# S5 boundary states stored contiguous by chunk, and some second copies moved from ScalarE to VectorE

## The chip, the cores and the metric

The kernel runs on one core of a Trainium2 chip. The metric is the device time of one execution in microseconds, as the median over several runs. TensorE (PE) multiplies matrices, VectorE (DVE) and ScalarE (ACT) work element by element, GpSimd (POOL) does so too and starts DMAs, SyncE (SP) starts most of the DMAs. In the profile PE stands for products, PEld for the loading of their stationary matrices.

## The reference, cut to what matters

A backbone of two layers is applied to 128 context tokens and 256 latent tokens. Each layer is half a SwiGLU feed-forward, a token mixer, and half a feed-forward. The mixer of the first layer is an S5 state-space layer: 64 groups of 16 channels, each with 64 complex states, scanned in both directions.

```python
def s5_mixer(h, p, j, init):
    ...
    u = (h @ w_in[j]).astype(F32)
    ug = u.reshape(bt, l, S5_GROUPS, S5_GROUP)
    for d, rev in ((0, False), (1, True)):
        abr, abi, bbr, bbi = s5_discretize(...)
        ...
        sr, si = s5_direction(ug, abr, abi, bbr, bbi, s0, rev)   # s[t] = A s[t-1] + B u[t]
    ...
    y = (jnp.einsum('blgp,gip->blgi', s_re, c_re[j].astype(F32))
         - jnp.einsum('blgp,gip->blgi', s_im, c_im[j].astype(F32)))
    y = y.reshape(bt, l, D_MODEL) + d_skip[j].astype(F32) * u
    y = jax.nn.gelu(y).astype(h.dtype)
    a, g = jnp.split(y @ w_glu[j], 2, axis=-1)
    out = a * jax.nn.sigmoid(g)
```

## The kernel before, in words

All activations lie with channels on the partitions and tokens on the free axis, 384 tokens side by side. Large products are split into a high and a low part (`hi` by ACT, `lo` by DVE) and take three products each, at lines L263 to L265; their weights come through seven buffers `raw` of 512 KB that SP loads in the written order (`fetched`, L245).

The S5 mixer cuts the tokens into chunks of 8: 16 of the context, 32 of the latents, and one column of zeros between them, so `NC_` = 49 chunk columns. The work has these steps.

1. The input projection gives U, [(t, j), group, chunk], by way of DRAM (`ud`), with DMAs that POOL starts.
2. `inputs(b)`, L861, multiplies U by a matrix for each group; ACT and DVE copy the results into `sb`, [state, slot, re/im, group], in an order in which both directions run forward (rows 0 to 63 are the forward direction, 64 to 127 the backward one).
3. `steps` (L878 to L881) runs the recurrence over chunks in `sb`, 32 steps of four operations for three blocks of groups: DVE takes groups 0 to 23, then 40 to 63, and POOL 24 to 39. DVE's two blocks are written as one loop, the third block starting 22 steps after the first.
4. `direct(m)`, L909, multiplies a chunk's own inputs and puts the result of eight groups in one bank of PSUM. `m` counts the eight groups of groups. `twice` lets each product write a second time into columns that are not used.
5. `align` copies boundary states from `sb` into `al[m]`, eight groups to a tile: `first_part(m)` what the first sixteen steps give, `second_part(m)` the rest, two copies of 240 and 528 columns on 64 partitions each. All are on ACT (`on_act`); the profile gives them L847, the line of `on_act`. In `al` the columns are [chunk, re/im, group], so a group's 49 chunks lie 16 floats apart.
6. `outputs(m)`, L918, adds the states' part to the bank: 16 products of 64 columns (`CP`), each multiplied twice, so 128 columns. The columns past 49 belong to padding that POOL sets to zero (L890). Then ACT applies the Gelu (L921), and its queue writes y to DRAM (`yd`). This is called y(m) below.
7. `fetch` brings y back by channel, and `split` makes `hh` (ACT, L945) and `hl` (DVE, L947), the input of the GLU product, whose first six weights are split beside y(5) to y(7) and behind.

The order of DVE, ACT and SP in this part is written out by hand: all of `inputs`, all of `direct`, the loop of the recurrence, and then one list of parts, where f is a first part, s_ a second part, y an `outputs`:

```python
for part, m in ((f, 0), (f, 1), (f, 2), (s_, 0), (s_, 1), (y, 0), (s_, 2), (f, 3), (f, 4), (y, 1),
                (s_, 3), (y, 2), (f, 5), (s_, 4), (y, 3), (f, 6), (f, 7), (s_, 5), (y, 4),
                (s_, 6), (y, 5), (s_, 7), (y, 6), (y, 7)):
```

Behind each y(m) of that list stand two more loads of matrices, the `fetch` of y(m-1), the `split` of y(m-3), behind y(5) and y(6) the splitting of GLU weights, and behind y(2) and y(3) a few products of the modulation of a later layer (L143 on TensorE, summed by DVE). Each engine runs its instructions in order.

Of the kernel before, what the change touches and what calls it, by code (L numbers as in the profile page):

```python
# [16 lines left out]
D = 1024  # L17
# [6 lines left out]
Q = 8  # L24
# [20 lines left out]
def backbone(ctx, tc, a, o):  # L45
# [41 lines left out]
    def ada_chunks():  # L87
        """Pieces of the modulation's weights: for TensorE in groups of (kind, pair of tiles) that are transposed
        together, for VectorE by tiles."""
        for l in range(2):  # L90
            for s in range(3):
                groups = [[(0, tp), (1, tp)] for tp in range(4)] if (l, s) == (0, 0) else \
                    [[(kind, tp) for tp in range(4)] for kind in (0, 1)]
                for group in groups + [[(2, tp) for tp in range(4)]]:
                    if (l, s, group[0][0]) in ADA_VEC:
                        vec_todo.extend((l, s, group[0][0], t) for t in range(KT))
                        continue
                    for j in range(len(group)):
                        for kh in range(2):
                            yield l, s, group, j, kh  # L100
# [10 lines left out]
    def ada_room(pool, bufs):  # L111
        """More buffers for pieces loaded ahead, for a while."""
        assert not any(x[2] for x in ada_loaded)
        ada_extra[:] = pool, bufs, 0

    def ada_load(cap=99, q=nc.gpsimd):
        """Loads ahead, up to cap pieces."""
        while ada_todo and len(ada_loaded) < min(cap, ADA_BUFS + ada_extra[1]):
            extra = ada_extra[2] < ada_extra[1]
            pool = ada_extra[0] if extra else adp  # L120
            w = pool.tile([128, 4, 256], F32, name="adaw", tag="adaw", bufs=ada_extra[1] if extra else ADA_BUFS)
            ada_extra[2] += extra
            c = ada_todo.pop(0)
            l, s, group, j, kh = c
            kind, tp = group[j]
            q.dma_start(w, a["ada_w"][l, s, kind * 4 + tp, kh])  # L126
            ada_loaded.append((c, w, extra))

    def ada_fill(n=1, load=True, bank=psaux, flush=True):
        """The products of n loaded pieces of the modulation's weights, then the next loads. Those of a group's  # L130
        item j come in rows 2 j, 2 j + 1 of each quarter, which holds a quarter of the sum."""
# [24 lines left out]
    def vec_pool():  # L156
        """For a while, what ada_vec needs."""
        st = ExitStack()
        vec[3] = vp = phase(st, "vec")
        vec[:2] = vp.tile([128, 2, D], F32, name="cb"), vp.tile([128, 256], mybir.dt.bfloat16, name="dump")  # L160
        nc.sync.dma_start(vec[0], bass.AP(a["condr"].tensor, 0, [[0, 128], [1, 2 * D]]))
        S.activation(vec[0], vec[0], AF.Silu)
        return st

    def ada_vec():
        """A tile of the modulation on VectorE: sums over a quarter of the rows each, then of those."""
# [103 lines left out]
    def pairs(w, n, xh, xl, at={}):  # L270
        """Column-tile pairs (a, g) of products with K = 1024; the tiles of one call go k by k.
        at[k], if given, is called before the products of row tile k."""
# [14 lines left out]
    def singles(w, n, xh, xl, at={}):  # L287
        """Single column tiles of one product with K = 1024; the tiles of one call go k by k."""
        ps = [psum() for _ in w]
        for k in range(KT):  # L290
            if k in at:
                at[k]()
            for i, t in enumerate(w):
                mm3(ps[i][:, :n], t, k * 128, xh[:, k, :n], xl[:, k, :n], k == 0, k == KT - 1)
        return ps

# [1 line left out]
    def params(i, t0=0, t1=KT, out=None):  # L298
        """Affine of norm i - 1 with the shift and scale of sub-layer i, for tiles t0 .. t1."""
# [24 lines left out]
    class Norm:  # L324
        """Norm i of r. Its input's products with the next weights start before the statistics are known:
        W (rs (r - mu) g' + b') = rs (W (g' r)) - rs mu (W g') + W b', for the tiles that come first."""
# [18 lines left out]
        def add(self, m):  # L345
            """Row tile m of r is final."""
# [19 lines left out]
        def pre(self, load, group, srcs, n, then):  # L366
            """The first products of the next sub-layer, n sources at a time, with the statistics in between;
            the weights of the products that follow."""
# [53 lines left out]
        def rest(self):  # L422
            """The input of the next sub-layer, split in hh and hl, and ALPHA * x in r."""
# [8 lines left out]
        def final(self):  # L432
            """The norm itself, to the output."""
# [15 lines left out]
        def apply(self, ps):  # L449
            """The norm on the product of ph, pl in ps, but for its column bias: (tile, biases)."""  # L450
# [97 lines left out]
    # State rows are (direction, p). A backward state's chunks are taken in reverse.  # L548
# [11 lines left out]
    def vexp(out, x, k, p):  # L560
        """exp(x) on the vector engine, to float32's last bits; x, k and p are overwritten."""
# [17 lines left out]
    def s5_tables(gp_):  # L579
        """Generator of the steps that build the chunk matrices."""  # L580
# [13 lines left out]
        # sine and cosine of ang, by quadrant  # L594
# [33 lines left out]
        # powers 0 .. 8 of A  # L628
# [22 lines left out]
        # q = (A - 1) / a  # L651
# [18 lines left out]
        # pe[s]: power 7 - s (forward), s (backward); pg: powers 0 .. 8, - (forward), -, 8 .. 0 (backward)  # L670
# [11 lines left out]
        def build_e(ch):  # L682
# [7 lines left out]
            # bb = q b  # L690
# [4 lines left out]
            # E: [g][ri][s][j]  # L695
# [7 lines left out]
        def build_g(ch, bc, ncr):  # L703
            """C A^e: [g][ri][slot][i]"""
# [26 lines left out]
        def taps(ch, bb, Gt):  # L731
            """[j][slot][i], slots 0 .. 7 backward (lag 7 .. 0), 7 .. 14 forward (lag 0 .. 7), and D"""
# [35 lines left out]
    def beside(slots, n, soon=0, nvec=0):  # L768
        """Work beside the products, called at each of so many slots: n pieces of the modulation on TensorE, evenly
        after the first ones, or, before those, nvec on VectorE, and steps of the S5 tables."""  # L770
# [19 lines left out]
    def s5(i, prev):  # L790
        l, s3 = divmod(i, 3)
        with ExitStack() as st:
            sa = phase(st, "s5a")
            # CP columns or more, as many as cost no more than NC_, are multiplied: those past NC_ are not used,
            # and where they reach into the next result's place that result overwrites them
# [43 lines left out]
            with ExitStack() as st2:  # L839
# [9 lines left out]
                def inputs(b):  # L849
                    """Each chunk's own part of the states: slot c + 1, backward chunks in reverse."""  # L850
# [19 lines left out]
                def steps(E, g0, n):  # L870
                    """The recurrence over chunks for n groups, operation by operation."""
# [11 lines left out]
                # boundary states by chunk, eight groups to a tile  # L883
                al = {}

                def al_tiles():
                    for m in range(8):
                        p_, tag = ((hip, "hi"), (lop, "lo"))[m % 2]
                        al[m] = p_.tile([128, 1024], F32R, name="al", tag=tag).bitcast(F32)
                        G.memset(al[m][:, NC_ * 16:], 0.0)  # L890

                def align(copy, m, c0, n, s0, dr, d):
                    """States d of chunks c0 .. c0 + n from slots s0, s0 + dr, .."""
                    copy(vw(al[m], c0 * 16, [[16, n], [8, 2], [1, 8]], 64 * d, 64),
                         vw(sb, s0 * 128 + m * 8, [[128 * dr, n], [64, 2], [1, 8]], 64 * d, 64))

                def twice(py, g, n):
                    """Group g's place in a bank and one that is not used, for the same again: TensorE's clock stays
                    up, and the columns of the matrices take as long to load."""
                    return vw(py, g * NC_, [[512 - CP - g * NC_, 2], [1, n]])  # L900

                def direct(m):
                    """The part of y from its own chunk: [(t, i), g, c], eight groups to a bank."""
# [9 lines left out]
                def outputs(m, py, gt):  # L913
                    """The states' part of y, and back to channels by tokens."""
                    for g in range(8):
                        for ri in range(2):
                            c0 = ((g % 4) * 2 + ri) * 128
                            PE.matmul(twice(py, g, CP), gt[g // 4][:, c0:c0 + 128],  # L918
                                      vw(al[m], ri * 8 + g, [[0, 2], [16, CP]]), start=False, stop=g == 7 and ri == 1)
# [9 lines left out]
                with tc.manual_schedule(engines={ET.Pool}):  # L929
                    proj(1, False, al_tiles)  # L930
                    with tc.manual_schedule(engines={ET.DVE, ET.Activation, ET.SP}):
                        py, yc = {}, {}

                        def first_part(m):
                            """What the first sixteen steps give of the boundary states."""
# [3 lines left out]
                        def second_part(m):  # L939
                            align(on_act, m, 34, 15, 34, 1, 0)  # L940
                            align(on_act, m, 16, 33, 49, -1, 1)
# [90 lines left out]
    def lru_params():  # L1032
# [6 lines left out]
        # softplus(-lam) = max(-lam, 0) + log1p(exp(-|lam|))  # L1039
# [20 lines left out]
    def lru(i, prev):  # L1060
# [11 lines left out]
        def conv(m, t, b=None):  # L1072
            """Centred convolution along each sequence: the first tap."""
# [5 lines left out]
        def taps(m, t):  # L1079
            """The other taps."""  # L1080
# [37 lines left out]
        def scan(mm, E=V):  # L1118
            w, A, B = ([x[mm, d] for d in range(2)] for x in (W, R, GI))
            # 1 - A^2 = tanh(4 softplus r) (1 + A)^2  # L1120
# [158 lines left out]
    def enter(tp, part=None):  # L1279
        """Rows 2 tp, 2 tp + 1 of the first input, in two parts."""  # L1280
# [14 lines left out]
    def first(load):  # L1295
        """The first products, as their weights, the input and its modulation come in."""
# [123 lines left out]
```

## Time and profile before

| what | value |
|---|---|
| time, median of three runs | 1669.81 us (1669.69 to 1672.33) |
| span of the profiled execution | 1665.7 us |
| TensorE busy, products | 1579.2 us (95%) |
| VectorE busy | 1255.1 us (75%) |
| ScalarE busy | 701.7 us (42%) |
| GpSimd busy | 349.3 us (21%) |
| moved by DMA | 301.23 MB, 181 GB/s on average |

The span is the time from the first to the last instruction of the one execution that was profiled; the device time has some 4 us more around it. A busy share is an average over stages with different limits. A row of a group of instructions has the line, the engine, the operation, output and inputs by name, the shapes, the number, busy time, mean duration in ns, and the idle time of the engine just before with what ended it. A row in order of time has the start, the duration, engine and line, and in brackets the idle time before it.

### The profile page before, as it was taken

What the parts mean: (1) busy time and instruction counts of PE and PEld (TensorE: products, weight loads), DVE (VectorE), ACT (ScalarE), POOL (GpSimd) and SP (SyncE); (2) the same over time, 40 slices, a digit from 0 to 9 for tenths busy, and PEclk for the clock granted to TensorE, in tenths of its full rate; (3) what the DMA queues carried; (4) which work ended last, traced back from release to release, by engine and by line L of the source; (5) the groups of instructions that cost most, each with busy time, mean ns of one, the idle gap of its engine ahead of it and who ended that gap; (6) DMA issues with size and microseconds to landing.
All of it is one profiled execution on the core that took longest, in us unless ns stands there. A gap on an engine that the chain in (4) does not pass through costs nothing.

```text
span 1665.7 us, 26476 instructions
## 1 busy us (share of the span) xinstructions
PE 1579.2 (95%) x9690; PEld 1495.3 (90%) x9690; DVE 1255.1 (75%) x3093; ACT 701.7 (42%) x1166; POOL 349.3 (21%) x553
## 2 busy tenths in 40 slices
PE   6989999999889999999999999999999689999996
PEld 5877987899878998999999999999987589999996
DVE  4999999977583478978769997884587979744444
ACT  4422332346433456333336532333459466333332
POOL 0145445433480004000000400000154513000001
PEclk9999999999989999999999999999999899999997
DMA  9676776875676742757546365654614353544321
GB/s 349 250 229 213 246 237 231 269 242 223 128 261 183 244 140 94 235 173 238 177 138 199 120 200 175 228 182 122 215 64 153 114 165 124 171 148 139 103 75 38
DMA packets 100867, 301.23 MB, mean 181 GB/s; under 512 B 20320, under 2 KB 32096, under 8 KB 100480
## 3 DMA queue, kind: packets, MB, share of 16 engines
q1 hardware_dynamic: 83920, 242.80, 45.0%
q0 software_dynamic: 15664, 55.12, 10.3%
q8 instruction: 76, 1.25, 0.3%
q10 hardware_dynamic: 1152, 1.61, 0.3%
q14 instruction: 55, 0.45, 0.1%
HBM read 275.89 MB, written 27.80 MB: 182 GB/s over the span
## 4 chain that ended last, share of the span: by engine, by line
PE 71%; DVE 18%; DMA 4%; issue 3%; POOL 2%; ACT 2%; SPq 0%; ACTq 0%; DVEq 0%; POOLq 0%
PE mm L263 21%; PE mm L264 21%; PE mm L265 20%; PE mm L918 3%; DVE lo L255 2%; DVE hl L316 1%; PE mm L861 1%; DMA adaw<-in_ada_w 1%; DMA ud<-s5stg 1%; PE aux L143 1%; DVE s5tp L641 1%; PE aux L918 1%; DVE r L427 1%; DVE lxc L1085 1%; DMA s5U<-ud 1%
## 5 line engine op out<-in xcount | busy, mean ns | idle before, releaser
L263 PE MATMUL mm<-hh,hi 128*128 128x384 f32 (+1 forms) x1632 | 561.4, 344 | 12.4 <-DVE hh L1138 5.3
L264 PE MATMUL mm<-hl,hi 128*128 128x384 f32 (+1 forms) x1632 | 555.3, 340 | 14.1 <-DVE hl L316 13.9
L265 PE MATMUL mm<-hh,lo 128*128 128x384 f32 (+1 forms) x1632 | 554.1, 340 | 0.3 <-DVE lo L255 0.3
L255 DVE TENSOR_TENSOR lo<-raw,hi 128x1024 fp32r<-128x1024 f32 (+1 forms) x344 | 390.8, 1140 | 185.7 <-ACT hi L252 179.2
L252 ACT ACTIVATE hi<-raw 128x1024 fp32r<-128x1024 f32 (+1 forms) x332 | 322.2, 975 | 492.3 <-PE mm L264 447.1
L263 PEld LDWEIGHTS mm<-hh,hi 128*128 128x128 f32 x1632 | 308.5, 189 | 30.9 <-issue 16.7
L264 PEld LDWEIGHTS mm<-hl,hi 128*128 128x128 f32 x1632 | 308.5, 189 | 20.3 <-DVE hl L316 19.8
L265 PEld LDWEIGHTS mm<-hh,lo 128*128 128x128 f32 x1632 | 308.4, 189 | 0.8 <-DVE lo L255 0.8
L263 PE MATMUL mm<-zh,hi 128*128 128x384 f32 x704 | 243.7, 346 | 6.0 <-ACT zh L475 6.0
L264 PE MATMUL mm<-zl,hi 128*128 128x384 f32 x704 | 239.5, 340 | 0.5 <-DVE zl L476 0.5
L265 PE MATMUL mm<-zh,lo 128*128 128x384 f32 x704 | 239.1, 340 | 0.0
L263 PEld LDWEIGHTS mm<-zh,hi 128*128 128x128 f32 x704 | 133.2, 189 | 16.2 <-issue 8.8
L264 PEld LDWEIGHTS mm<-zl,hi 128*128 128x128 f32 x704 | 133.3, 189 | 1.5 <-DVE zl L476 1.5
L265 PEld LDWEIGHTS mm<-zh,lo 128*128 128x128 f32 x704 | 133.2, 189 | 0.0
L178 DVE SCALAR_TENSOR_TENSOR dump<-raw,cb 128x256 bf16<-128x256 f32 x256 | 108.5, 424 | 27.1 <-DMA raw<-in_ada_t 26.2
L475 ACT ACTIVATE zh<-w 128x384 fp32r<-128x384 f32 x88 | 46.0, 524 | 183.4 <-DVE w L483 179.6
L178 DVE SCALAR_TENSOR_TENSOR raw<-raw,cb 128x256 f32<-128x256 f32 x256 | 108.4, 424 | 5.6
L126 POOL DMA_DIRECT2D adaw<-in_ada_w x55 | 31.4, 571 | 309.4 <-PE aux L143 286.6
L391 POOL TENSOR_TENSOR t<-mv 128x3 f32<-128x3 f32 x5 | 4.1, 814 | 385.0 <-ACT mv L390 385.0
L540 DVE SCALAR_TENSOR_TENSOR r<-mm,gate,r 128x128 f32<-128x128 f32 (+1 forms) x144 | 53.3, 412 | 24.5 <-PE mm L265 24.3
L429 POOL TENSOR_SCALAR r<-r,lag,lab 128x384 f32<-128x384 f32 x40 | 65.5, 1651 | 24.1 <-ACT w L321 24.0
L476 DVE TENSOR_TENSOR zl<-w,zh 128x384 fp32r<-128x384 f32 x88 | 53.2, 608 | 19.2 <-ACT zh L475 19.0
(357 smaller groups left out, 2039.9 us busy)
## 6 DMA issues: line engine op xcount, KB each, us to landing
raw<-in_up SPq DMA_DIRECT2D x176, 512.0 KB, 4.4
raw<-in_ada_t SPq DMA_DIRECT2D x64, 512.0 KB, 3.9
raw<-in_down SPq DMA_DIRECT2D x56, 512.0 KB, 3.6
adaw<-in_ada_w POOLq DMA_DIRECT2D x55, 512.0 KB, 5.1
adaw<-in_ada_w SPq DMA_DIRECT2D x25, 512.0 KB, 8.1
raw<-in_down SPq DMA_DIRECT2D x48, 192.0 KB, 2.4
gd<-s5G POOLq DMA_DIRECT2D x16, 512.0 KB, 4.6
etd<-s5eo POOLq DMA_DIRECT2D x16, 512.0 KB, 5.5
```

What stands on the lines that cost most here:

```text
L126: q.dma_start(w, a["ada_w"][l, s, kind * 4 + tp, kh])
L178: V.scalar_tensor_tensor(out, wq, 1.0, cb[:, g, q * 256:q * 256 + 256], op0=OP.mult, op1=OP.mult, accum_out=part[:, t, g, q:q + 1])
L252: S.activation(hi[:, :n], raw[:, :n], AF.Copy)
L255: V.tensor_tensor(lo[:, :n], raw[:, :n], hi[:, :n], op=OP.subtract)
L263: PE.matmul(ps, hi[:, c:c + 128], xh, start=start, stop=False)
L264: PE.matmul(ps, hi[:, c:c + 128], xl, start=False, stop=False)
L265: PE.matmul(ps, lo[:, c:c + 128], xh, start=False, stop=stop)
L429: G.tensor_scalar(r[:, k, :], r[:, k, :], lag[:, i, k:k + 1], lab[:, i, k:k + 1], op0=OP.mult, op1=OP.add)
L475: S.activation(zh, z, AF.Copy)
L476: V.tensor_tensor(zl, z, zh, op=OP.subtract)
L540: V.scalar_tensor_tensor(r[:, m, c0:c1], ps[:, c0:c1], gate[:, m, g:g + 1], r[:, m, c0:c1], op0=OP.mult, op1=OP.add)
L918: PE.matmul(twice(py, g, CP), gt[g // 4][:, c0:c0 + 128], vw(al[m], ri * 8 + g, [[0, 2], [16, CP]]), start=False, stop=g == 7 and ri == 1)
```

## The change

`al` is laid out as [re/im, group, chunk], so the 49 chunks of a group lie side by side; `align` stores accordingly. `outputs` multiplies 49 columns, twice, instead of 64, twice, and the padding with its memsets is gone. The second copies of m = 3 to 7 are done by VectorE instead of ScalarE, at the same places of the written order. All other lines of the diff take out comments.

```diff
                 def al_tiles():
                     for m in range(8):
                         p_, tag = ((hip, "hi"), (lop, "lo"))[m % 2]
                         al[m] = p_.tile([128, 1024], F32R, name="al", tag=tag).bitcast(F32)
-                        G.memset(al[m][:, NC_ * 16:], 0.0)
 
                 def align(copy, m, c0, n, s0, dr, d):
-                    copy(vw(al[m], c0 * 16, [[16, n], [8, 2], [1, 8]], 64 * d, 64),
+                    copy(vw(al[m], c0, [[1, n], [8 * NC_, 2], [NC_, 8]], 64 * d, 64),
                          vw(sb, s0 * 128 + m * 8, [[128 * dr, n], [64, 2], [1, 8]], 64 * d, 64))
...
                 def outputs(m, py, gt):
                     for g in range(8):
                         for ri in range(2):
                             c0 = ((g % 4) * 2 + ri) * 128
-                            PE.matmul(twice(py, g, CP), gt[g // 4][:, c0:c0 + 128],
-                                      vw(al[m], ri * 8 + g, [[0, 2], [16, CP]]), start=False, stop=g == 7 and ri == 1)
+                            PE.matmul(twice(py, g, NC_), gt[g // 4][:, c0:c0 + 128],
+                                      vw(al[m], (ri * 8 + g) * NC_, [[0, 2], [1, NC_]]), start=False,
+                                      stop=g == 7 and ri == 1)
...
                         def second_part(m):
-                            align(on_act, m, 34, 15, 34, 1, 0)
-                            align(on_act, m, 16, 33, 49, -1, 1)
+                            copy = on_act if m < 3 else V.tensor_copy
+                            align(copy, m, 34, 15, 34, 1, 0)
+                            align(copy, m, 16, 33, 49, -1, 1)
```

## Rows read from the trace of the kernel before

**Rows 1.** The page: span, and the chain's lines.

```profile
span 1665.7 us, 26476 instructions
...
PE mm L263 21%; PE mm L264 21%; PE mm L265 20%; PE mm L918 3%; DVE lo L255 2%; DVE hl L316 1%; PE mm L861 1%; DMA adaw<-in_ada_w 1%; DMA ud<-s5stg 1%; PE aux L143 1%; DVE s5tp L641 1%; PE aux L918 1%; DVE r L427 1%; DVE lxc L1085 1%; DMA s5U<-ud 1%
```

**Rows 2.** Three stretches: busy us of PE, PEld, DVE, ACT, POOL; clock, DMA.

```profile
475.00:494.00 19.00, 19.00 (x139) 16.45 (x139) 16.70 (x82) 6.41 (x14) 16.57 (x63) 1.00 0.91 320
494.00:515.00 21.00, 21.00 (x98) 19.59 (x96) 16.45 (x86) 7.35 (x13) 7.25 (x28) 1.00 0.63 194
...
539.00:553.00 14.00, 14.00 (x67) 13.24 (x65) 4.72 (x5) 5.83 (x9) 0.00 (x0) 1.00 0.74 210
```

**Rows 3.** The chain in order of time: start, us, what.

```profile
475.62 1.96 PE mm L909 x16
...
494.13 20.96 PE mm L918 x96
515.09 1.86 PE mm L143 x32
516.96 7.16 PE mm L918 x32
...
539.26 13.97 PE aux L918 x64
```

**Rows 4.** PE in order of time, the products of `inputs`.

```profile
432.51 4.93 PE L861 MATMUL mm<-s5U,s5e 128*128 128x128 f32 x28 [1.99 <-DMA s5U<-ud]
...
442.50 14.04 PE L861 MATMUL mm<-s5U,raw 128*128 128x128 f32 x124
465.09 10.12 PE L861 MATMUL mm<-s5U,raw 128*128 128x64 f32 x68 [8.56 <-DMA s5U<-ud]
```

**Rows 5.** One microsecond after the gap at 430.5: PE busy, clock.

```profile
433.00:434.00 1.00, 1.00 (x7) 0.50 0.63 42
```

**Rows 6.** Groups by form, 415 to 620 us: copies of states.

```profile
L847 ACT ACTIVATE s5sb<-mm 64x392 f32<-64x392 f32 x16 | 13.0, 853 | 13.0 <-PE mm L861 12.5
...
L847 ACT ACTIVATE al<-s5sb 64x528 f32<-64x528 f32 x8 | 5.1, 640 | 1.2 <-DVE s5sb L881 1.1
...
L847 ACT ACTIVATE s5sb<-mm 64x128 f32<-64x128 f32 x10 | 3.9, 389 | 0.1
...
L868 DVE COPY s5sb<-mm 64x256 f32<-64x256 f32 x6 | 3.5, 591 | 0.0
...
L847 ACT ACTIVATE al<-s5sb 64x240 f32<-64x240 f32 x8 | 3.2, 399 | 12.2 <-DVE s5sb L881 11.2 <-ACT s5Y L921 0.9
...
L867 DVE COPY s5sb<-mm 64x128 f32<-64x128 f32 x6 | 2.3, 385 | 2.2 <-ACT s5sb L847 2.2
```

**Rows 7.** ACT in order of time, from the first y to the sixth.

```profile
493.14 1.72 ACT L847 ACTIVATE al<-s5sb 64x528 f32<-64x528 f32 x3 [1.12 <-DVE s5sb L881]
...
501.16 0.50 ACT L921 ACTIVATE s5Y<-mm 128x392 f32<-128x392 f32 x1 [5.00 <-PE mm L918]
...
502.07 1.05 ACT L847 ACTIVATE al<-s5sb 64x240 f32<-64x240 f32 x2 [0.42 <-ACT s5Y L921]
...
540.20 0.53 ACT L945 ACTIVATE hh<-s5stg 128x392 fp32r<-128x392 f32 x1 [0.40 <-ACT s5Y L921]
540.64 1.04 ACT L252 ACTIVATE hi<-raw 128x1024 fp32r<-128x1024 f32 x1
```

**Rows 8.** DVE in order of time: last step of the recurrence, a split.

```profile
511.73 0.21 DVE L881 TENSOR_TENSOR s5sb<-s5sb,w 128x48 f32<-128x48 f32 x1
...
540.77 0.57 DVE L947 TENSOR_TENSOR hl<-s5stg,hh 128x392 fp32r<-128x392 f32 x1 [6.40 <-ACT hh L945]
541.71 1.23 DVE L255 TENSOR_TENSOR lo<-raw,hi 128x1024 fp32r<-128x1024 f32 x1 [0.38 <-ACT hi L252]
```

**Rows 9.** POOL in order of time, around the memsets.

```profile
449.78 1.99 POOL L890 MEMSET al<- 128x240 f32 x8
458.70 0.57 POOL L835 DMA_DIRECT2D s5U<-ud  x1 [6.93 <-DMA ud<-s5stg]
```

## Prediction

> **What bounds the kernel now.** I read the page first: TensorE's products hold most of the chain that ended last, and the line the change rewrites, L918, is on it with 3% in `mm` and 1% in `aux` [rows 1]. Time saved there is time of the kernel, as long as nothing else is late. [...]
>
> The chain in order of time gives the pitch [rows 3]. Each of the eight results y(m) of `outputs` is 16 products, recorded as 32 instructions. 96 of them took 20.96 us, so 0.218 us each and 6.99 us for one y. The products of `direct`, L909, took 1.96 us for 16, or 0.1225 us each. From the first L918 (494.13) to the last (539.26 + 13.97 = 553.23) are 59.1 us, with two short runs of L143 between.
>
> Why are L918's so slow? They multiply 128 columns, each 16 floats (64 bytes) from the last. L909 multiplies 98 adjacent columns, writes through the same `twice` into two places of a bank, and adds to what is there. L861 multiplies up to 128 adjacent columns, and 124 of its instructions took 14.04 us, 0.113 each, at full clock [rows 4]. So neither the count of columns nor the second writing explains 0.218; the distance between columns does. The new L918 has L909's form exactly: two runs of 49 adjacent columns.
>
> **TensorE's part.** 32 x 0.1225 = 3.92 us instead of 6.99 for each y, 3.07 less, and 8 x 3.07 = 24.6 us in all. That is the most that can come back. What follows takes a part of it away.
>
> **The start.** The first y waits for the second copies of m = 0, still on ACT; the longer of them begins at 493.14 [rows 7], when DVE's first block ends. Its new store puts adjacent values 49 floats apart. ACT's nearest row for scattered stores is L847 into `s5sb` (128 floats apart): 389 ns for 128 columns, 853 for 392, so 1.76 ns per column above 164 ns; the copy in place now took 640 ns for 528 columns [rows 6]. By the scattered row it takes 164 + 528 x 1.76 = 1.09 us (ends: 0.64, as now, and 1.5, with 1.43 times the slope as in rival 1) and ends at 494.23. TensorE starts at about 494.35, 0.2 us later than now. ACT's other copies before y3 (each pair 1.7 us or so instead of 1.04) lie under three y of 3.92 us and cost nothing.
>
> **The gap before y(3).** Three y end at 494.35 + 11.76 = 506.1, and the 32 instructions of L143 (1.86 us [rows 3]) at 508.0. y(3) needs its second copies, which the change moves from ACT to VectorE. DVE runs in the written order and these stand behind its last recurrence step, which starts at 511.73 and takes 0.21 [rows 8]. Now that wait costs nothing, since y(3) begins at 516.96 [rows 3]. After the change it is what is late next. DVE's nearest row is its copy with scattered stores, L868 and L867: 591 ns for 256 columns, 385 for 128, or 1.61 ns per column above 179 [rows 6]. The two copies of 240 and 528 columns then take 0.57 + 1.03 = 1.60 us. The lower end is 1.0: what ACT pays now for runs of 8, 0.40 + 0.64, or half of DVE's 1.61 per column; the upper end is 2.1 (rival 1). I take 1.60, because it is the same engine and the same kind of store. y(3) starts at 511.94 + 1.60 + 0.1 = 513.65, after 5.65 us of idle TensorE.
>
> **The clock after it.** After the 8.56 us gap at 465.09, 68 instructions took 10.12 us [rows 4]; at 0.113 they would take 7.70, so 2.4 us went. [...] A gap of 5.65 us stands between the two: I charge 2.0 (ends 0 and 2.4). y(3) ends at 513.65 + 3.92 + 2.0 = 519.6, and 16 instructions of L143 (half of 1.86) later y(4) begins, at 520.5.
>
> **The rest.** y(4) ends at 524.4, y(5) at 528.4, y(6) at 532.3, if their copies are there. On DVE the order behind the first wait is: sums of the modulation, copies(4), hl(0), copies(5) after y(3), hl(1), copies(6) after y(4), hl(2), the first GLU weight's `lo`, copies(7) after y(5). Each hl waits for ACT's Gelu of that y, 0.91 us to the next ACT operation, and for `hh`, 0.53 [rows 7]; then hl takes 0.57 [rows 8]. Copies(4) end near 516, copies(5) at 519.6 + 0.1 + 0.91 + 0.53 + 0.57 + about 0.4 + 1.60 = 523.7 (needed 524.4), copies(6) at 528.2 (needed 528.4). These are hidden, with less than 1 us to spare. Copies(7) are not: after y(5) come 0.1 + 0.91 + 0.53, then `hi` 1.04 on ACT, `lo` 1.23 on DVE [rows 7, 8], then 1.60, with 0.2 of handing over. That is 534.0, and y(7) was due at 532.3. It ends at 534.0 + 3.9 = 537.9. The gap of 1.7 us may pull the clock down once more: 0 to 1.8, the loss after the 1.99 us gap; taken as 0, since it is shorter.
>
> **What costs nothing.** The eight memsets of `al` (1.99 us on POOL) lie in a wait for the DMA of `ud` that lasts 6.93 us [rows 9]; without that cover they would have been 2.0 us on the path to U. The moved copies issue no DMA and pass no other queue; SP's loads of `gd` and GLU weights wait for the y that frees a buffer, so they come earlier as y does. First copies of m = 5 to 7 stay on ACT, 1.8 us a pair, before Gelu(4).
>
> **The sum.** 553.2 - 537.9 = 15.3 us. Behind the stage TensorE again leads the chain, and waits there follow from earlier work of the same chain, so I let it all pass through. The profiled span is 1665.7 [rows 1], 4.1 below the median of 1669.81; I take these 4.1 as unchanged. 1669.8 - 15.3 = 1654.5.
>
> [...] No row here shows a step of 49 floats. [...]
>
> **Rivals.** (1) Scattered copies are dearer. At 1.43 times the row's 1.61 per column, 179 + 240 x 2.3 and 179 + 528 x 2.3 make 2.1 us a pair. y(3) moves by 0.5 and copies(7) by as much again: y(7) ends at 539.0, and the kernel takes 1655.6. No row has this step, so none excludes it; against it, ACT's and DVE's slopes at 128 floats lie close together, 1.76 and 1.61. 0.20.
>
> (2) The distance is not the whole cause and the change only shortens the stream, 128 to 98 columns: 0.218 x 98/128 = 0.167 an instruction, 5.35 us a y. y(2) and L143 end at 512.3, y(3) runs from 513.65 to 519.0 with the clock kept, and four more, 0.9 later, end at 541.3: 1657.9. L909 and L861 speak against it. 0.10.
>
> (3) DMA takes over. The engines are busy 0.74 of 14.00 us for two y [rows 2], so 5.2 us of their time a y, more than 3.92. If no load were ahead, four y at 5.2 behind 520.5 end at 541.3: 1657.9. Against it: seven buffers are filled ahead and TensorE's gap lets them fill. 0.10.
>
> (4) Cheap copies, no lost clock: 1.0 us a pair. y(3) starts at 513.0, y(5) ends at 525.7, copies(7) are there at 530.7, y(7) ends at 534.6: 1651.2. 0.06.
>
> (5) Slower than before: the clock sits at its lower level through the whole stage, because shorter products load TensorE less. At double pitch a y is 7.84 us; eight from 494.35 with 5.7 of L143 end at 562.8, 9.6 later: 1679.4. It decides from about y(2) on: with the low clock only from y(3) the end is 555, about as before (1671.6). L909, of the same form, kept 1.00 over 19 us [rows 2]. 0.02 for the whole, 0.02 from y(3) on.
>
> **How the numbers follow.** Forecast 0.50, the rivals 0.20, 0.10, 0.10, 0.06, 0.02, 0.02. The low end, 1651.0, is rival 4; the high end is rivals 2 and 3 with some 1.5 us for a second fall of the clock or a loss behind the stage: 1659.5. A difference of 0.2% (3.3 us) is about what a measurement of this kernel can tell from none. Faster: 0.50 + 0.20 + 0.10 + 0.10 + 0.06 = 0.96; same 0.02; slower 0.02.
>
> **What would show it.** L918 at 98 columns and near 0.12 us in the chain; TensorE idle some 5 to 6 us before y(3), released by DVE's copies behind the last L881; a granted clock of 0.50 there; a second gap before y(7); the first GLU product near 538 instead of 553. It is wrong if L918's pitch stays above 0.15, if DVE's copies take over 2.1 us a pair, or if the GLU products wait.

## The result

The changed kernel takes 1650.7 us (median of four runs, 1649.87 to 1655.82) against 1670.1 us before: a ratio of 0.9889, with a 95% interval of 0.9874 to 0.9903, so 16 to 21 us less. The forecast was 1654.5 with a range from 1651.0 to 1659.5: right in sign and mechanism, some 4 us too slow, and the median stands 0.3 us below the low end. A second measurement of the same kernel, below, gave 1651.9 and a ratio of 0.9899 [0.9864, 0.9935].

In the changed file L908 is the old L909 (`direct`), L917 the old L918 (`outputs`), L893 the copy on VectorE inside `align`, L946 and L948 the old L945 and L947; L847 stays. First TensorE in order of time (start, us, instructions, idle time before and what ended it), from the first y to the first GLU product; it answers to [rows 3].

```profile
492.00 10.96 PE L917 MATMUL mm<-al,raw 128*128 128x98 f32 x96 [0.74 <-ACT al L847]
502.89 1.93 PE L143 MATMUL mm<-adaw,cond 128*32 128x256 f32 x32
510.83 5.76 PE L917 MATMUL mm<-al,raw 128*128 128x98 f32 x32 [6.00 <-DVE al L893]
516.52 1.07 PE L143 MATMUL mm<-adaw,cond 128*32 128x256 f32 x16
517.52 7.39 PE L917 MATMUL mm<-al,raw 128*128 128x98 f32 x64
524.93 3.78 PE L917 MATMUL aux<-al,raw 128*128 128x98 f32 x32
529.83 3.78 PE L917 MATMUL aux<-al,raw 128*128 128x98 f32 x32 [1.11 <-ACT s5Y L921]
533.39 0.42 PE L263 MATMUL mm<-hh,hi 128*128 128x392 f32 x1
```

The same view of the kernel before:

```profile
493.97 21.12 PE L918 MATMUL mm<-al,raw 128*128 128x128 f32 x96
...
552.89 0.53 PE L263 MATMUL mm<-hh,hi 128*128 128x392 f32 x1
```

Three y take 10.96 us where they took 21.12. Then TensorE is idle for 6.00 us, which VectorE's copies end; y(3) takes 5.76 us, where an undisturbed y such as y(6) takes 3.78; y(7) starts after another gap of 1.11 us. From the first y to the first GLU product, called the stage from here on, it is now 533.39 - 492.00 = 41.4 us. Before it was 552.89 - 493.97 = 58.9, so 17.5 us less.

The same stretch by windows (busy us of PE, PEld, DVE, ACT, POOL; granted clock, DMA share, GB/s), for [rows 2]:

```profile
492.00:503.00 11.00, 11.00 (x100) 10.90 (x104) 10.17 (x49) 9.39 (x11) 6.97 (x28) 1.00 0.82 265
503.00:505.00 2.00, 1.82 (x32) 0.82 (x30) 1.83 (x12) 1.40 (x2) 0.00 (x0) 1.00 1.06 207
505.00:511.00 6.00, 0.17 (x1) 0.17 (x2) 5.49 (x29) 0.87 (x2) 0.00 (x0) 0.76 0.85 283
511.00:516.50 5.50, 5.50 (x32) 5.42 (x32) 1.75 (x4) 0.00 (x0) 0.00 (x0) 0.64 0.32 107
```

The shorter products keep the clock at 1.00. In the gap VectorE is the busy engine (5.49 of 6.00 us), and behind it the clock averages 0.64 while y(3) runs, against 1.00 everywhere in [rows 2]. VectorE in order of time around the gap and before y(7), for [rows 8]:

```profile
509.45 0.21 DVE L881 TENSOR_TENSOR s5sb<-s5sb,w 128x48 f32<-128x48 f32 x1
509.58 1.20 DVE L893 COPY al<-s5sb 64x240 f32<-64x240 f32 x2
...
527.39 1.22 DVE L255 TENSOR_TENSOR lo<-raw,hi 128x1024 fp32r<-128x1024 f32 x1 [0.42 <-ACT hi L252]
528.53 1.19 DVE L893 COPY al<-s5sb 64x240 f32<-64x240 f32 x2
```

The copies for y(3) start the moment the last recurrence step ends, and y(3) starts 0.05 us after them. Those for y(7) stand behind the `lo` of a GLU weight, as forecast, and end at 529.72, 0.11 us before y(7) starts; the Gelu that the profile names as what ended this wait (L921) had ended at 529.25. Last the copies by form (mean ns behind the busy time), for [rows 6]:

```profile
L847 ACT ACTIVATE al<-s5sb 64x528 f32<-64x528 f32 x3 | 3.4, 1129 | 0.9 <-DVE s5sb L881 0.8
L893 DVE COPY al<-s5sb 64x528 f32<-64x528 f32 x5 | 3.2, 633 | 0.1
L893 DVE COPY al<-s5sb 64x240 f32<-64x240 f32 x5 | 2.8, 550 | 0.0
L847 ACT ACTIVATE al<-s5sb 64x240 f32<-64x240 f32 x3 | 1.9, 627 | 10.1 <-DVE s5sb L881 9.6 <-ACT s5Y L921 0.4
```

On ACT the new store costs 1129 ns where the old one cost 640; on VectorE a pair takes 1.2 us.

### The profile page after: what moved, and what is told of

Read it like the earlier page. It is cut to its first block, busy times and chain, and to the rows that moved or that the text cites. A ratio compares the mean times of both kernels' runs of the same rounds, so it can differ in the third digit from the quotient of the medians.

```text
span 1648.1 us, 26477 instructions
## 1 busy us (share of the span) xinstructions
PE 1561.0 (95%) x9690; PEld 1479.4 (90%) x9690; DVE 1260.2 (76%) x3103; ACT 706.5 (43%) x1156; POOL 348.7 (21%) x545
## 4 chain that ended last, share of the span: by engine, by line
PE 55%; DVE 8%; POOL 2%; issue 1%; ACT 1%; DMA 0%; SPq 0%; ACTq 0%; DVEq 0%
PE mm L263 18%; PE mm L264 18%; PE mm L265 18%; DVE hl L316 1%; DVE lxc L1086 1%; DVE lo L255 1%; PE mm L1101 1%; DVE r L427 1%; DVE r L426 1%; DVE lxc L1130 1%; DVE lW L1130 1%; PE aux L418 0%; DVE lG L1125 0%; PE aux L384 0%; DMA adaw<-in_ada_w 0%
## 5 line engine op out<-in xcount | busy, mean ns | idle before, releaser
L476 DVE TENSOR_TENSOR zl<-w,zh 128x384 fp32r<-128x384 f32 x88 | 51.9, 592 | 19.1 <-ACT zh L475 18.9
```

The source lines that it names most:

```text
L476: V.tensor_tensor(zl, z, zh, op=OP.subtract)
```

## Experiments: is it the distance, or the number of columns?

The theory: TensorE reads its moving columns slowly when they lie far apart in SBUF. The rival: the 64 columns with their padding cost, 128 against 98. Three kernels separate them.

**The old layout with 49 columns instead of 64** (e4).

```diff
-                            PE.matmul(twice(py, g, CP), gt[g // 4][:, c0:c0 + 128],
-                                      vw(al[m], ri * 8 + g, [[0, 2], [16, CP]]), ...)
+                            PE.matmul(twice(py, g, NC_), gt[g // 4][:, c0:c0 + 128],
+                                      vw(al[m], ri * 8 + g, [[0, 2], [16, NC_]]), ...)
```

> The kernel before with 49 columns written twice in outputs instead of 64, still 16 floats apart. Theory (the distance between columns sets the pace): time per column stays 1.70 ns, so L918 goes from 0.218 to 0.167 us and the stage is 13 us shorter: about 1657 us. Rival (what costs is the 64 columns with their padding): the pitch falls to 0.114, as after the change, and the stage by 25 us: about 1645 us.

Measured: 1655.77 us, ratio 0.9915 [0.989, 0.9939]. TensorE in order of time, the first three y:

```profile
494.50 16.39 PE L918 MATMUL mm<-al,raw 128*128 128x98 f32 x96
```

16.39 / 96 = 0.171 us, still 1.7 ns per column. With 98 columns 16 floats apart an instruction takes half as long again as with 98 adjacent ones (10.96 / 96 = 0.114). The stage takes 46.2 us (540.70 - 494.50), 12.7 less than before. The theory holds; fewer columns are a gain only because far columns are slow.

**128 adjacent columns** (e6). The changed kernel with 64 places for each group in `al`, and the padding's memsets back.

```diff
-                    copy(vw(al[m], c0, [[1, n], [8 * NC_, 2], [NC_, 8]], 64 * d, 64),
+                    copy(vw(al[m], c0, [[1, n], [8 * CP, 2], [CP, 8]], 64 * d, 64),
...
-                            PE.matmul(twice(py, g, NC_), gt[g // 4][:, c0:c0 + 128],
-                                      vw(al[m], (ri * 8 + g) * NC_, [[0, 2], [1, NC_]]), ...)
+                            PE.matmul(twice(py, g, CP), gt[g // 4][:, c0:c0 + 128],
+                                      vw(al[m], (ri * 8 + g) * CP, [[0, 2], [1, CP]]), ...)
```

> As the changed kernel, but each group has 64 adjacent places in al, 15 of them set to zero by POOL, and outputs multiplies 64 columns twice: 128 columns, as before the change, now adjacent. Theory (distance): L917 stays near 0.114 us (L861 has 0.113 with up to 128 adjacent columns), first to last about 41.5 us, the time within 3 us of 1650.7. Rival (the columns count too): 128/98 of 0.114, 0.149 us, a y of 4.8 us; the stage 3 to 5 us longer than after the change, as its gap before y(3) hides the first three.

TensorE in order of time, the first three y:

```profile
494.37 10.96 PE L918 MATMUL mm<-al,raw 128*128 128x128 f32 x96 [0.48 <-POOL s5sb L880]
```

10.96 us, to the hundredth what 98 adjacent columns take. Something else than the stream sets 0.114; the loading of the stationary matrix, 192 ns an instruction and busy 10.90 of 11.00 us in the windows above, is the candidate, but no run took it away. The single run took 1655.45 us, beyond the 3 us I had allowed: its first y came 2.4 us later than in the changed kernel, and its stage of 43.8 us lost 2.4 more, at y(7), where TensorE waited 1.91 us for a GLU weight and y(7) then took 5.44 us instead of the 3.81 of y(6).

**One kernel with seven distances** (e5). Each y(m) reads its 49 columns at another distance; the rest is the variant called e3 below. Its columns are not the states, so only its times count.

```diff
+                    d = (1, 2, 4, 8, 16, 3, 5, 1)[m]
+                    b = min(49, (783 - 48 * d) // 15)
...
-                                      vw(al[m], (ri * 8 + g) * NC_, [[0, 2], [1, NC_]]), ...)
+                                      vw(al[m], (ri * 8 + g) * b, [[0, 2], [d, NC_]]), ...)
```

> As e3_vector_from_5, but the 49 columns that outputs(m) reads are 1, 2, 4, 8, 16, 3, 5 and 1 floats apart for m = 0 to 7, taken from the same tile, so they are not the states they should be. All else, the number of columns too, is the same. Theory (distance): at 1 the pitch is 0.114 us, at 16 it is 0.167, as in e4_old_layout_98; in between it rises with the distance, and a step at which neighbours no longer lie together in memory shows where. [...] Rival (only very wide steps cost): 2, 3, 4, 5 and 8 all stay at 0.114 to 0.125 and only 16 is slow.

TensorE in order of time, in windows that cut out one y each: distances 2, 4, 8, 16, 3 and 5.

```profile
498.25 3.62 PE L919 MATMUL mm<-al,raw 128*128 128x98 f32 x31
501.71 5.79 PE L919 MATMUL mm<-al,raw 128*128 128x98 f32 x32
509.29 5.97 PE L919 MATMUL mm<-al,raw 128*128 128x98 f32 x32
516.20 5.62 PE L919 MATMUL mm<-al,raw 128*128 128x98 f32 x32
521.78 4.29 PE L919 MATMUL mm<-al,raw 128*128 128x98 f32 x31
525.90 5.87 PE L919 MATMUL aux<-al,raw 128*128 128x98 f32 x32
```

Less the length of the last product (0.27 to 0.36), an instruction takes 0.112 us at distance 2, 0.133 at 3, 0.175 at 4, 0.178 at 5, 0.181 at 8 and 0.170 at 16. A distance of 2 floats costs nothing here, 4 already costs as much as 16, and what lies between 4 and 16 costs no more. Since 128 adjacent columns take no longer than 98, a small price at a distance of 2 could be hidden under the 0.112 that something else sets. Why the time rises between 2 and 4 floats no run shows.

## Experiments: what did the copies on VectorE do?

**The move without the layout** (e2). The kernel before, with the copies of m = 3 to 7 on VectorE.

```diff
                         def second_part(m):
-                            align(on_act, m, 34, 15, 34, 1, 0)
-                            align(on_act, m, 16, 33, 49, -1, 1)
+                            copy = on_act if m < 3 else V.tensor_copy
+                            align(copy, m, 34, 15, 34, 1, 0)
+                            align(copy, m, 16, 33, 49, -1, 1)
```

> The old layout with the second copies of m = 3 to 7 on VectorE. Theory: nothing waits for them at the old pitch of 6.99 us a y, since y(3) begins at 517 and VectorE is free at 512; L918 keeps 0.218 us; within 0.2% of the kernel before. Rival (the move itself brings part of the gain): 3 us or more faster than before.

Measured: 1670.77 us, ratio 1.0005 [0.9992, 1.0018]. The first three y on TensorE, and VectorE's copies by form:

```profile
494.77 21.18 PE L918 MATMUL mm<-al,raw 128*128 128x128 f32 x96 [0.48 <-POOL s5sb L881]
...
L894 DVE COPY al<-s5sb 64x528 f32<-64x528 f32 x5 | 3.5, 699 | 0.1
...
L894 DVE COPY al<-s5sb 64x240 f32<-64x240 f32 x5 | 1.3, 270 | 0.0
```

Three y take 21.18 us as before and no gap opens behind them. The move by itself brings nothing.

**The layout without the move** (e1). The changed kernel with every second copy on ACT.

```diff
-                            copy = on_act if m < 3 else V.tensor_copy
+                            copy = on_act
```

> The new layout of al with all second copies left on ACT, as before. Theory (the layout pays, the move to VectorE costs): y(3) no longer waits for VectorE's last recurrence step, so TensorE's 6 us gap before y(3) and the low clock behind it are gone; ACT is late instead with copies(5), after first copies of m = 6 and 7, by some 3 us. From the first L917 to the end of the last 35 to 36 us (41.5 after the change), about 1645 us. Rival (the move relieves ACT): ACT's scattered stores, 1.75 us a pair, are late for every y from y(3) on; the stage takes 45 us or more, 1654 us or more.

Measured: 1647.65 us, ratio 0.987 [0.9846, 0.9893]. TensorE and then ACT in order of time:

```profile
506.21 3.81 PE L917 MATMUL mm<-al,raw 128*128 128x98 f32 x32
...
517.47 6.57 PE L917 MATMUL mm<-al,raw 128*128 128x98 f32 x32 [2.70 <-ACT al L847]
...
512.07 5.35 ACT L847 ACTIVATE al<-s5sb 64x544 f32<-64x544 f32 x6
```

The wait of y(3) is gone, as the theory said. But ACT does six scattered copies in a row, 5.35 us, before y(5), TensorE waits 2.70 us there, and y(5) behind this gap takes 6.57 us instead of 3.81. First y to first GLU product: 38.5 us, not the 35 to 36 I expected, since I had charged nothing for slower products behind a gap. So all of the gain comes from the layout (with it, the 49 columns), and the move as written brought nothing: without it the stage is 2.9 us shorter, and the median 3 us below that of the changed kernel, though the intervals overlap (0.9846 to 0.9893 and 0.9874 to 0.9903).

**VectorE only where its own recurrence makes the states** (e3), m = 5 to 7; m = 3 and 4 come from POOL, which is done earlier.

```diff
-                            copy = on_act if m < 3 else V.tensor_copy
+                            copy = on_act if m < 5 else V.tensor_copy
```

> The new layout; second copies on VectorE only for m = 5 to 7, whose states VectorE's own last block makes; m = 3 and 4, whose states come from POOL, stay on ACT. Theory: no wait of y(3) and y(4) for VectorE, no low clock in the stage, and ACT is not late either: first to last L917 in 33 to 34 us, about 8 us less than after the change, 1643 us. Rival (the gap before y(3) is slack that is given back behind the stage, by GLU weights or DMA): the stage is shorter but the time stays within 2 us of 1650.7.

Measured: 1649.34 us, ratio 0.9868 [0.9841, 0.9894]; the stage 38.1 us. The 33 to 34 us were not reached. TensorE before y(7), ACT and VectorE ahead of it:

```profile
527.45 5.41 PE L917 MATMUL aux<-al,raw 128*128 128x98 f32 x32 [3.33 <-ACT hi L252]
...
523.93 1.06 ACT L252 ACTIVATE hi<-raw 128x1024 fp32r<-128x1024 f32 x1 [2.76 <-DMA raw<-in_s5glu]
...
525.01 1.23 DVE L255 TENSOR_TENSOR lo<-raw,hi 128x1024 fp32r<-128x1024 f32 x1 [3.24 <-ACT hi L252]
526.16 1.19 DVE L893 COPY al<-s5sb 64x240 f32<-64x240 f32 x2
```

Six y run without a pause of over 0.2 us, faster than the loads follow. Then ACT waits 2.76 us for the first GLU weight, VectorE's `lo` waits for ACT's `hi`, the copies for y(7) stand behind `lo`, and TensorE waits 3.33 us. Behind that gap y(7) takes 5.41 us, at a granted clock of 0.51 from 528 to 530 us. And why was the weight late? SP's waits in this stretch (us in all, times, longest):

```profile
SPq L926 <- DMA yd<-s5Y: 14.3, 3, 8.3
SPq L245 <- DMA yd<-s5Y: 10.1, 4, 4.7
```

SP issues in the written order, and there the loads of weights (L245) stand behind the `fetch` of y (L926), which waits for y to be written. That this order made the weight late is read from these waits and not shown by a run of its own.

**Copies ahead of everything** (e7). The copies of m = 5 to 7 on VectorE, the first ones of 6 and 7 too, right behind the last recurrence step.

```diff
-                        (s_, 3), (y, 2), (f, 5), (s_, 4), (y, 3), (f, 6), (f, 7), (s_, 5), (y, 4),
-                        (s_, 6), (y, 5), (s_, 7), (y, 6), (y, 7)):
+                        (s_, 3), (y, 2), (f, 5), (s_, 4), (s_, 5), (f, 6), (s_, 6), (f, 7), (s_, 7), (y, 3), (y, 4),
+                        (y, 5), (y, 6), (y, 7)):
```

> As e3_vector_from_5, with the second copies of m = 5 to 7 and the first copies of m = 6 and 7 on VectorE right behind its last recurrence step, ahead of y(3) in the written order, so that no copy stands behind a GLU weight's lo or a Gelu. Theory (in e3 y(7) waited 3.3 us for copies that stood behind a split whose weight came late): no gap left in the stage but under 0.5 us, first to last L917 in 33 us instead of 38, 1645 us. Rival (DMA and the GLU weights end last anyway): the stage is 33 us, but GLU products wait for weights and the time stays at 1648 to 1650.

Measured: 1643.21 us, ratio 0.9839 [0.9818, 0.9861]: better than both kernels. TensorE in order of time:

```profile
491.64 10.96 PE L917 MATMUL mm<-al,raw 128*128 128x98 f32 x96 [0.26 <-ACT al L847]
...
504.63 3.81 PE L917 MATMUL mm<-al,raw 128*128 128x98 f32 x32 [0.17 <-ACT al L847]
...
509.38 7.39 PE L917 MATMUL mm<-al,raw 128*128 128x98 f32 x64
516.60 7.31 PE L917 MATMUL aux<-al,raw 128*128 128x98 f32 x64
523.69 0.43 PE L263 MATMUL mm<-hh,hi 128*128 128x392 f32 x1
```

The stage takes 32.05 us, no gap in it is over 0.2, and no GLU product waits for a weight. Against this order the changed kernel's copies cost 41.4 - 32.05 = 9.3 us of the stage, made of the two gaps (6.00 and 1.11), the clock behind the first one (2.0) and 0.2 of smaller pieces; against copies left on ACT (e1) they cost 2.9. VectorE's copies by form:

```profile
L893 DVE COPY al<-s5sb 64x544 f32<-64x544 f32 x2 | 1.3, 650 | 0.1
L893 DVE COPY al<-s5sb 64x256 f32<-64x256 f32 x2 | 0.8, 385 | 0.1
```

**The fetch of y on POOL's queue** (e8), on top of that.

```diff
-                    nc.sync.dma_start(yc, by_channel(yd, m))
+                    nc.gpsimd.dma_start(yc, by_channel(yd, m))
```

> As e7_copies_first, with the loads of y by channel issued by POOL instead of SP, so that SP's loads of matrices no longer stand behind a wait for the writing of y (10 us in e3). Theory: the GLU weights come 2 to 3 us earlier and the first GLU products don't wait; 1 to 2 us faster than e7, 1643 to 1644 us. Rival (the DMA engines themselves are full, 0.9 to 1.1 in that stretch of e3): earlier issues only wait longer; the same as e7.

Measured: 1644.53 us, ratio 0.985 [0.9836, 0.9864], no faster than without it. Its stage is 32.05 us, the same. In e7's order no product had waited for the loads any more, so the loss that I meant to win back was not there; here two waits of 0.6 us for the split of GLU weights even appear behind the stage. SP's loads now wait 24.1 us (20.0 and 4.1) for products of `outputs`, against 7.7 (6.5 and 1.2) in e7. So this run does not show that the `fetch` made e3's weight late. Nor does it say whether the DMA engines are full.

## Experiments: the price of a scattered store, and the change once more

**Copies by the distance of their stores** (e9). Extra copies behind the last y of the changed kernel, from 64 partitions of `sb` into a spare tile; a size marks a form.

```diff
+                        forms = [(8, [32, 16, 1], 16), (8, [32, 16, 1], 4), (8, [64, 32, 2], 15), (8, [96, 48, 3], 14),
+                                 (8, [128, 64, 4], 13), (8, [128, 1, 8], 12), (8, [2, 1, 16], 11), (8, [2, 1, 49], 10),
+                                 (8, [2, 1, 63], 9), (15, [2, 1, 49], 7), (9, [32, 16, 1], 16)]
...
+                                    copy(vw(xt, 0, [[f1, n], [f2, 2], [f3, k]], 64, 64),
+                                         vw(sb, 1 * 128, [[32, n], [16, 2], [1, k]], 64, 64))
```

> As the changed kernel, with extra copies on VectorE and then on ACT behind the last y: 64 partitions of sb, adjacent columns, into a spare tile with stores 1, 2, 3, 4, 8, 16, 49 and 63 floats apart (each size occurs once), each twice. They feed nothing; the time is longer by them. Theory of the prediction (a scattered store costs the 1.61 ns per column of the copy from PSUM on VectorE, 1.76 on ACT): from a step of 2 or 4 on VectorE pays 1.6 ns per column, ACT 1.76. [...]

The kernel took 1658.15 us with them. Groups by form (mean ns): distance 4 is 208 columns, 49 is 160, 2 is 240, 1 is 256 and 64.

```profile
L847 ACT ACTIVATE xt<-s5sb 64x208 f32<-64x208 f32 x2 | 1.2, 587 | 0.1
...
L847 ACT ACTIVATE xt<-s5sb 64x160 f32<-64x160 f32 x2 | 1.0, 498 | 0.1
...
L847 ACT ACTIVATE xt<-s5sb 64x240 f32<-64x240 f32 x2 | 0.9, 432 | 0.1
L847 ACT ACTIVATE xt<-s5sb 64x256 f32<-64x256 f32 x2 | 0.8, 414 | 0.1
...
L999 DVE COPY xt<-s5sb 64x208 f32<-64x208 f32 x2 | 0.7, 356 | 0.1
...
L999 DVE COPY xt<-s5sb 64x160 f32<-64x160 f32 x2 | 0.6, 319 | 0.1
...
L999 DVE COPY xt<-s5sb 64x256 f32<-64x256 f32 x2 | 0.6, 292 | 0.1
L999 DVE COPY xt<-s5sb 64x240 f32<-64x240 f32 x2 | 0.6, 285 | 0.1
L847 ACT ACTIVATE xt<-s5sb 64x64 f32<-64x64 f32 x2 | 0.5, 252 | 0.1
L999 DVE COPY xt<-s5sb 64x64 f32<-64x64 f32 x2 | 0.4, 193 | 0.1
```

VectorE: (292 - 193) / 192 = 0.52 ns per column above 160 for adjacent stores, so (319 - 160) / 160 = 1.0 at 49 and 0.94 at 4. ACT: 0.84 above 198, so 1.9 at 49 and at 4. At 2 VectorE costs what it costs at 1, ACT 0.98. On VectorE the theory of that run falls in these copies: 0.5 adjacent and about 1.0 scattered, not 1.6. On ACT the row was near. My row copies from PSUM and at 128 floats; no run separates the source from the distance.

The kernel's own copies do not all follow these prices. With scattered stores, 544 columns (650 ns), 256 (385, both e7) and 528 (633) lie near 160 + 0.9 a column, but 240 take 550, which is 1.6 a column. With adjacent stores (e2), 240 take 270, as here, but 528 take 699, more than scattered.

**The changed kernel again** (e10).

> The changed kernel once more. If the stage alone makes the difference, its first to last L917 takes 41 to 42 us again and the time is 17 to 18 us below the kernel before; what the first profile showed beyond that, a first y 2 us earlier and a tail 2 us longer, should move from run to run.

Measured: 1651.9 us. TensorE's gap before y(3) is 5.92 us, that before y(7) 1.98, y(3) takes 6.31, and the stage 42.7 us (534.09 - 491.36). The expectation on the stage was missed by 0.7, and the time, 18.9 us below the kernel before, by 0.9. First y and tail, the time from the first GLU product to the end, hardly moved between the two profiles of the changed kernel: the first y starts at 492.00 and 491.36, the tail is 1114.7 and 1114.6 us. Over the kernels they do move: in the eleven other profiles of this study, the one before included, the first y starts between 491.6 and 496.8, at 493.25 in e9, whose edit lies behind it; the tail is 1111 to 1117 us in all but e9. So that they move from run to run is borne out for the first y only, by e9.

## Why the prediction was right, and where it was off

**TensorE's part.** The mechanism is shown: distance, not columns. The size was off. I took 0.1225 us from L909's 1.96 us for 16, and that piece of the chain begins with a product that follows the bank's clearing and is longer than the rest (0.35 us against a mean of 0.28 in the changed kernel). Over 96 in a row it is 0.114: 3.65 us a y, not 3.92, so 2.2 us over eight y, of which the three in front are hidden by the gap.

**The start.** ACT's scattered copy was priced at 1.09 us and took 1.13. TensorE waited for it, 0.74 us.

**The gap before y(3).** VectorE's order made y(3) wait, as forecast: 5.65 us forecast, 6.00 measured. Two errors cancel here: the three y in front were shorter than I said, and so were the copies. The copies are a mis-sized term, 1.60 us a pair against 1.20, and the error is all in one of the two: the 240 columns took 0.55 us for 0.57, the 528 columns 0.63 for 1.03. The row that I chose copies from PSUM, and the extra copies show that within SBUF VectorE can do a scattered store at two thirds of it; why only the longer copy of the pair did is open. Rival (1), that they are dearer than the row, falls: the extra copies take 1.0 ns per column at 49 floats and 0.9 at 16 (176 columns in 324 ns), and the kernel's dearest 1.6. The factor of 1.43 behind its 2.1 us a pair was a guess of mine; no row and no run shows it.

**The clock.** 2.0 us were charged, an estimate between the losses behind two gaps of [rows 4]: 2.4 us behind 8.56 us, and 4.93 - 28 x 0.113 = 1.8 behind 1.99 us, where the granted clock was 0.50 [rows 5]. In the changed kernel 5.76 - 3.78 = 2.0 were lost in the first profile, at the averaged 0.64, and 6.31 - 3.78 = 2.5 in the second, at 0.59 from 510 to 516.5 us. In e9 and e6, behind gaps of 6.11 and 6.14 us, it was 1.9 and 1.6.

**The rest.** Copies(4) to (6) were hidden, copies(7) were not, and the gap there was 1.11 us, then 1.98 in the second profile, for 1.7 forecast. In the first profile the clock was 1.00 behind it (529 to 533.4 us), and y(7) took 3.78 and 3.79 us in the two. I had taken the loss as 0 because the gap is short, and here this was partly luck: behind a gap of 1.56 us at the same place in e9 and one of 1.91 in e6 y(7) took 5.41 and 5.44 us, 1.6 to 1.7 more, while the gap of 1.98 in e10 cost nothing. The length of the gap alone does not decide it. y(7) in e9:

```profile
531.52 5.41 PE L917 MATMUL aux<-al,raw 128*128 128x98 f32 x32 [1.56 <-ACT hh L946]
```

**The sum.** Forecast 15.3 us; the stage gave 17.5 in the first pair of profiles and 16.2 with the second of the changed kernel. Counted from the first y, TensorE is 2.2 us ahead of the forecast at the end of the stage: 0.5 before y(3), 1.1 in the five y from there on, 0.6 in the smaller gap before y(7). In the first pair all of the stage's gain passed through to the end, as forecast: the spans are 1665.7 and 1648.1, 17.6 apart; a first y 2.0 us earlier and a tail 1.9 us longer cancel.

The rest of the miss is the 4.1 us between span and median, which the section on time and profile calls some 4 us around the span, and which I took as unchanged. In every run whose span is recorded beside its time, the two are 1.7 to 1.8 us apart. So the profiled execution of the kernel before took about 1667.5 us, an estimate from its span plus 1.8, and lay 2.6 below the median of 1670.1; that of the changed kernel, 1649.87, lay 0.8 below its own. This is why the medians differ by 17.6 + 2.6 - 0.8 = 19.4.

**The other rivals.** (2) falls with the kernel of 128 adjacent columns. (3), that DMA takes over, did not decide here, but it is near: in the order of e3 the first thing late was a weight, and the DMA share there is 0.87 to 1.10 in each 2 us from 516 to 530. (4) did not come true, since a pair took 1.2 us and not 1.0, and the clock was lost all the same; that its 1651.2 lies beside the measured 1650.7 is chance. (5) falls: three y at 1.00.

What I did not ask in the prediction was whether the move, which cost 2.9 us of the stage against copies left on ACT and 9.3 against the best order tried, was needed as it was written. I had found both gaps and priced them, and took them as given.

## What to carry to other kernels

Lay out a moving operand so that neighbouring columns are neighbours in SBUF, or at most two floats apart (98 columns took 0.112 to 0.114 us there and 0.17 to 0.18 from 4 floats on, e5), and let the copy that fills it pay for the scattering, where its engine has the time: in e1, at 5.35 us for six copies, ACT did not have it for every y, and TensorE waited 2.70 us. Before moving work to another engine, look at what stands ahead of it in that engine's order: here it was a recurrence that ended some 5 us after TensorE had run out of work. When a stage becomes faster, read the lists of waits again for each order of the copies: four placements of the copies gave stages of 41 to 43, 38.5, 38 and 32 us.

## What the runs showed of the hardware

- TensorE's moving columns, float32: 98 columns take 0.112 to 0.114 us at a distance of 1 or 2 floats, 0.133 at 3, and 0.17 to 0.18 from 4 to 16. 128 adjacent columns take no longer than 98: 10.96 us for 96 instructions of either (e6, changed kernel).
- Copies within SBUF, float32, in e9: VectorE 0.5 ns per column adjacent and 1.0 scattered, ACT 0.84 and 1.9. The copy from PSUM with scattered stores, 1.6 on VectorE [rows 6], is no safe measure for one within SBUF.
- One thing is open: in the changed kernel VectorE's copy of 240 columns took 550 ns and that of 528 only 633 at the same distance of stores, and with adjacent stores (e2) they took 270 and 699. They differ in direction of reading, in the start of the store and in the number of rows. Direction alone is not it, since 544 columns read forward (650 ns in e7) are as cheap by the column as the 528 read backward. No run separated the others.
- TensorE's granted clock averaged 0.64 behind the changed kernel's gap of 6.00 us, where y(3) took 5.76 us, and 1.00 behind that of 1.11, where y(7) took 3.78. Behind gaps of 1.56 and 1.91 us (e9, e6) y(7) took 5.41 and 5.44 us, behind one of 1.98 (e10) 3.79.
